# The opening of a hybrid RG-LRU / gMLP / ConvFFN layer: another order of loads, norms and first products

## The chip, the cores and the metric

One core of one Trainium2 chip runs the whole layer as one program. The metric is the device time of that program in microseconds, the median of several runs. Engines: PE is the matrix engine (PEld are its weight loads), DVE the vector engine, ACT the scalar engine, POOL the general engine, SP the engine from whose queue most transfers are issued.

## The reference, cut to what matters

One layer over 512 latent tokens and 256 context tokens of width 1024, all in float32. Only its beginning is touched by the change:

```python
def _rmsnorm(x, g):
    y = xf * lax.rsqrt(jnp.mean(xf * xf, axis=-1, keepdims=True) + EPS)
    return (y * g.astype(jnp.float32)).astype(x.dtype)

def _modulate(x, g, shift, scale):
    return _rmsnorm(x, g) * (1.0 + scale) + shift

m_x = (jax.nn.silu(c) @ w_mod[l] + b_mod[l]).reshape(B, N_MOD, 1, D_MODEL)
m_c = (jax.nn.silu(c_ctx) @ w_mod[l] + b_mod[l]).reshape(N_MOD, D_MODEL)
hc = _modulate(ctx, g_norm1[l], m_c[0], m_c[1])
pc = hc @ w_in[l][:, :W_R]                 # context: the 1280 recurrent columns only
hx = _modulate(x, g_norm1[l], m_x[:, 0], m_x[:, 1])
px = hx @ w_in[l]                          # latent: all 6912 columns
...                                        # convolution, gates, scans, gMLP, merge, FFN
```

So before the first product of the layer there have to be: the two vectors `c` and `c_ctx` put through silu and the first two blocks of `w_mod` (shift and scale), and the root mean square of each token. The latent scans start from the final context states, which is why the context products are wanted early too.

## The kernel before, in words

Tokens lie along the free axis and channels along the partitions, in 8 blocks (k = 0 to 7) of 128 channels: `xc[:, k, :]` holds 256 context tokens and then 512 latent tokens. Every large product is made in three passes: each float32 operand is split into a rounded high part and a rest (`wh`, `wl` for weights, `hxh`, `hxl` for the latent, `hch`, `hcl` for the context), and PE adds wh·xh, wh·xl and wl·xh in one PSUM bank. ACT casts the high part of a weight tile (line 93), DVE (POOL for some later tiles) subtracts to get the rest (line 95).

The order of instructions on each engine is made by a planner when the program is built: it takes what is ready by its own cost estimates, the earliest in program order first. `after(a, b)` adds an edge that only fixes the order of two instructions on one engine; it is no semaphore. A transfer waits in the queue of the engine that issues it; lines behind it on that queue wait too.

The opening, lines 214 to 348, goes as follows.

- Transfers from SP: the two condition rows (line 218), 1 MB of `w_mod` for block 0, the latent in eight pieces of 256 KB (line 228), the small parameters, `w_mod` for block 1, the first weight tile of two blocks, `w_mod` for block 2, the context, another weight tile, `w_mod` for block 3. POOL issues 512 KB of `c` spread over the partitions (`cbx`, line 352), which in the trace is its first transfer.
- `mod_cols(k)` (lines 257 to 273): 16 float32 matmuls of 128 columns on a quarter of the array's columns each give shift and scale of channel block k; ACT copies them out (line 268), one small matmul turns them (line 269), two DVE instructions add the bias and multiply by the norm's weight (lines 271 and 273). A float32 matmul stands in the trace as two instructions, so the 16 are 32.
- `norm_of` (lines 279 to 294): ACT squares each block, DVE adds the eight squares up (line 285), PE sums over the partitions with one matmul per 128 tokens against a column of ones (line 289), ACT takes the root, DVE the reciprocal, PE spreads the row over the partitions (line 203), ACT copies it to `rb` (line 294). First the latent, then the context.
- `mod_h(k, n)` (lines 325 to 330): DVE multiplies a block by scale and `rb`, ACT adds the shift and rounds to the high part, DVE makes the rest.
- The loop of lines 338 to 348: for each k, `mod_cols` and `mod_h` of block k + 2 (`LEAD = 2`) are issued ahead of the products of block k; the products are 18 passes of 512 latent columns into six banks (two `rx`, two `rg`, two `gr`) and 6 passes of 256 context columns into a shared bank (`rxc`).

Behind the loop the heads of the recurrent branch follow (`rx_head`, `gates_head`), whose first products are those of line 139. Weight tiles of 2 x 1024 columns go through two raw buffers and three pairs of split buffers for the whole kernel.

Of the kernel before, what the change touches and what calls it, by code (L numbers as in the profile page):

```python
# [10 lines left out]
F32 = mybir.dt.float32  # L11
F32R = mybir.dt.float32r
# [25 lines left out]
LEAD = 2  # L38
# [14 lines left out]
class Weights:  # L53
# [3 lines left out]
    def __init__(self, tc, raw, hl, ahead):  # L57
        self.tc, nc = tc, tc.nc
        self.nc, self.raw, self.hl, self.ahead = nc, raw, hl, ahead
        self.boost = 0  # L60
        self.units = []
        self.blocks = []
        self.loaded = 0
        self.split = 0
        self.taken = 0
        self.tiles = {}

# [8 lines left out]
    def load(self, u):  # L76
        while self.loaded <= u:
            src, n = self.units[self.loaded]
            t = self.raw.tile([P, 2 * BLK], F32, tag="raw", name=f"raw{self.loaded}")
            self.nc.sync.dma_start(t[:, :n], src)  # L80
            self.tiles[self.loaded] = t
            self.loaded += 1
        return self.tiles[u]

    def prepare(self, upto):
        nc = self.nc
        while self.split <= min(upto, len(self.blocks) - 1):
            u, at, n, on_pool, extra = self.blocks[self.split]
            r = self.load(u)[:, at : at + n]
            hl = self.extra if extra else self.hl  # L90
            h = hl.tile([P, BLK], F32R, tag="wh", name=f"wh{self.split}")
            l = hl.tile([P, BLK], F32R, tag="wl", name=f"wl{self.split}")
            nc.scalar.copy(h[:, :n], r)  # L93
# [14 lines left out]
def hybrid_block(ctx: ExitStack, tc: tile.TileContext, a: dict, out: bass.AP):  # L108
# [35 lines left out]
    for i in range(4):  # L144
        W.add(a["w_first"][i], [(4 + NFIRST) * P] * 2)
# [47 lines left out]

    def rstd_of(p, ss, tag, n=1, bias=None):
        r = p.tile([P, n], F32, tag=f"{tag}r", name=f"{tag}r", bufs=2)
        nc.scalar.activation(r, ss, AF.Sqrt, scale=1.0 / D, bias=eps if bias is None else bias)
        nc.vector.reciprocal(r, r)
        return r
# [14 lines left out]

    rx_ps, rg_ps = {}, {}

    with pool("pro", side="right") as pro:
        crow = pro.tile([2 * KD, P], F32, name="crow")
        nc.sync.dma_start(crow, a["c_row"])
        wms = {}

        def load_mod(k):
            wms[k] = pro.tile([P, 2, KD, P], F32, tag="wm", name=f"wm{k}", bufs=4)
            nc.sync.dma_start(wms[k].rearrange("p s k c -> p (s k c)"), a["w_mod01"][k])

        load_mod(0)
        xc = pro.tile([P, KD, TT], F32, name="xc")
        for k in range(KD):
            nc.sync.dma_start(xc[:, k, TC:], a["xc"][k])
        nc.sync.dma_start(sm, a["smalls"])
        load_mod(1)  # L230
        W.load(0)
        load_mod(2)
        nc.sync.dma_start(xc[:, :, :TC], a["ctx"].rearrange("p (k t) -> p k t", k=KD))
        W.load(1)
        load_mod(3)
# [6 lines left out]
        nc.gpsimd.memset(c32, 0.0)  # L242
        psc = mm_tile("psc")
        nc.tensor.transpose(psc[:, : 2 * KD], sig, ident[: 2 * KD, : 2 * KD])
        nc.vector.tensor_copy(c32[:, :, 0:2], psc[:, : 2 * KD].rearrange("p (n k) -> p k n", n=2))
        nc.vector.tensor_copy(sc, psc[:, :KD])
# [6 lines left out]
        nc.vector.tensor_copy(bm1[:, :, 0], col("bmod", 0, KD))  # L253
        nc.vector.tensor_scalar(bm1[:, :, 1], col("bmod", KD, KD), 1.0, None, op0=ALU.add)
        mss = {}

        def mod_cols(k):


            pm = aux_tile(f"pm{k}", 1)  # L260
            for kk in range(KD // 2):
                for s in range(2):
                    for h in range(2):
                        at = 64 * s + 32 * h
                        nc.tensor.matmul(pm[at : at + 32, :P], c32[:, 4 * h + kk, :], wms[k][:, s, 4 * h + kk, :],
                                         start=kk == 0, stop=kk == KD // 2 - 1, tile_position=(0, at))
# [3 lines left out]
            ms = mss[k] = pro.tile([P, 2, 2], F32, tag="ms", name=f"ms{k}", bufs=4)  # L270
# [5 lines left out]
        sqs = pro.tile([P, TT], F32, name="sqs")  # L276
        rb = pro.tile([P, TT], F32, name="rb")

        def norm_of(lo, hi):
            sq = lambda k: pro.tile([P, T], F32, tag="sq", name=f"sq{lo}{k}", bufs=4)[:, : hi - lo]  # L280
            nc.scalar.activation(sqs[:, lo:hi], xc[:, 0, lo:hi], AF.Square)
            for k in range(1, KD):
                q = sq(k)
                nc.scalar.activation(q, xc[:, k, lo:hi], AF.Square)
                nc.vector.tensor_tensor(sqs[:, lo:hi], sqs[:, lo:hi], q, op=ALU.add)
            n = (hi - lo) // P
            pss = aux_tile(f"pss{lo}", 0)
            for t in range(n):
                nc.tensor.matmul(pss[:, t : t + 1], sqs[:, lo + t * P : lo + (t + 1) * P], ones[:, 0:1],
                                 start=True, stop=True)  # L290
            r = rstd_of(pro, pss[:, :n], f"n1{lo}", n)
            prb = aux_tile(f"rb{lo}", 0)[:, : hi - lo]
            spread_rows(prb, r, n)
            return nc.scalar.copy(rb[:, lo:hi], prb)

        mod_cols(0)
        norm_of(TC, TT)
        mod_cols(1)
        normed = norm_of(0, TC)


        rxc = aux_tile("rxc", 0)
        gr_ps = {j: mm_tile(f"gr{j}") for j in range(NFIRST)}
        for j in range(2):
            rx_ps[j] = (mm_tile(f"rx{j}"), rxc[:, j * TC : (j + 1) * TC])
            rg_ps[j] = mm_tile(f"rg{j}")

        def products(k, wh, wl):
            xs = ((hxh[:, k, :], hxl[:, k, :]), (hch[:, k, :], hcl[:, k, :]))
            outs = [(rx_ps[j][0], j, *xs[0]) for j in range(2)] + [(rg_ps[j], 2 + j, *xs[0]) for j in range(2)]  # L310
            outs += [(gr_ps[j], 4 + j, *xs[0]) for j in range(NFIRST)] + [(rx_ps[j][1], j, *xs[1]) for j in range(2)]
            c0 = 4 + NFIRST
            for i, (o, j, xh, xl) in enumerate(outs):
                c = slice(j * P, (j + 1) * P)
                for n, (w, x) in enumerate(((wh, xh), (wh, xl), (wl, xh))):
                    first, last = k == 0 and n == 0, k == KD - 1 and n == 2
                    mm = nc.tensor.matmul(o, w[:, c], x, start=first and i != c0 + 1, stop=last and i != c0)
                    if (first or last) and i >= c0:
                        if i > c0:
                            after(mm, shared)  # L320
                        shared = mm

        PARTS = ((TC, TT, hxh, hxl), (0, TC, hch, hcl))

        def mod_h(k, n):
            lo, hi, dh, dl = PARTS[n]
            x, sh = xc[:, k, lo:hi], mss[k][:, n, 0:1]
            nc.vector.scalar_tensor_tensor(x, x, mss[k][:, n, 1:2], rb[:, lo:hi], op0=ALU.mult, op1=ALU.mult)
            nc.scalar.activation(dh[:, k, :], x, AF.Identity, bias=sh)
            nc.vector.scalar_tensor_tensor(dl[:, k, :], x, sh, dh[:, k, :].bitcast(F32), op0=ALU.add, op1=ALU.subtract)  # L330
# [3 lines left out]
        mod_h(0, 1)  # L334
        W.prepare(1)
        mod_h(1, 0)
        mod_h(1, 1)
        for k in range(KD):
            if k + 4 < KD:
                load_mod(k + 4)  # L340
            if k in (0, 2):
                W.load(k // 2 + 2)
            blk = W.take(ahead=1)
            if k + LEAD < KD:
                mod_cols(k + LEAD)
                mod_h(k + LEAD, 0)
                mod_h(k + LEAD, 1)
            products(k, *blk)

    W.boost = 1000  # L350

    nc.gpsimd.dma_start(cbx, a["c_b"])
# [20 lines left out]
    with pool("lamp") as lp:  # L373
# [4 lines left out]
        nc.vector.scalar_tensor_tensor(z, lam, -1.0, lam, op0=ALU.mult, op1=ALU.max)  # L378
# [270 lines left out]
    for k in range(KD):  # L649
        nc.gpsimd.dma_start(x1c[:, k, :], a["xc"][k])  # L650
# [207 lines left out]
def _layout(v):  # L858
# [7 lines left out]
    o["xc"] = f(np.asarray(v["x"][0]).T.reshape(KD, P, T))  # L866
# [66 lines left out]
```

## Time and profile before

| | us |
|---|---|
| median of 3 runs | 991.13 (991.07 to 996.96) |
| the profiled execution: its time | 989.86 |
| the profiled execution: its span | 988.1 |
| PE busy in the span | 951.6 (96%) |
| DVE busy | 665.2 (67%) |
| ACT busy | 478.0 (48%) |
| first product (line 317) starts | 24.68 |
| first product of the heads (line 139) starts | 75.51 |

"Busy" of PE counts every matmul until its modelled end, so that a busy PE can still be one that waits a little between passes. The span is what lies between the first and the last instruction; 1.8 us of the profiled time lie around it. A row of a timeline has start, duration, engine, line, what is written from what, the count of instructions merged, and in brackets the idle time of the engine before them with what ended it.

### The profile page before, as it was taken

The numbers are of one execution on the slowest core, as the hardware profiler recorded it, in microseconds if no ns is written. First come the engines' busy times: TensorE is split into PE (matmuls) and PEld (weight loads), VectorE is DVE, ScalarE is ACT, GpSimd is POOL, SyncE is SP. The second block draws the span as 40 slices with busy tenths as digits, with TensorE's granted clock in tenths as the row PEclk, the third lists the DMA queues.
The fourth block names the chain that finished last, engine by engine and source line by source line (L and its number), as shares of the span: only waits on it lengthen the run. The fifth ranks groups of instructions, "written<-read, shape, count | busy, mean of one in ns | idle before, by whom it ended". The sixth has DMA issues, their size and how long they took to land.

```text
span 988.1 us, 11916 instructions
## 1 busy us (share of the span) xinstructions
PE 951.6 (96%) x4787; PEld 789.4 (80%) x4787; DVE 665.2 (67%) x867; ACT 478.0 (48%) x661; POOL 95.0 (10%) x92
## 2 busy tenths in 40 slices
PE   3999999999999999999999998999999999999997
PEld 2788888888888788788888798888778888887686
DVE  3768496968574976586634456798886447888764
ACT  4546979786989552234222343443333213333333
POOL 0000000000000011100001031222220002222020
PEclk9999999999999999999999999999999999999999
DMA  9532212132222276734524331222213332221232
GB/s 355 223 134 86 78 51 86 43 107 86 86 86 86 86 257 233 257 148 175 198 97 170 111 125 43 86 86 86 85 43 108 105 128 86 85 86 64 84 109 86
DMA packets 23511, 116.85 MB, mean 118 GB/s; under 512 B 2576, under 2 KB 3744, under 8 KB 14368
## 3 DMA queue, kind: packets, MB, share of 16 engines
q1 hardware_dynamic: 17488, 94.59, 26.9%
q0 software_dynamic: 5968, 21.50, 6.2%
q8 instruction: 37, 0.61, 0.2%
q14 instruction: 18, 0.15, 0.1%
HBM read 113.98 MB, written 2.10 MB: 117 GB/s over the span
## 4 chain that ended last, share of the span: by engine, by line
PE 65%; DVE 16%; ACT 8%; issue 6%; DMA 3%; POOL 1%; SPq 0%; ACTq 0%; DVEq 0%; POOLq 0%
DVE acc L797 8%; PE d L140 4%; PE d L141 4%; PE d L139 4%; PE up L139 4%; PE up L141 4%; PE up L140 4%; DVE wl L95 2%; DMA wmod<-in_w_mod 2%; ACT wh L93 2%; PE pg L139 2%; PE pg L140 2%; PE pg L141 2%; PE gg L141 1%; PE gg L140 1%
## 5 line engine op out<-in xcount | busy, mean ns | idle before, releaser
L93 ACT CAST wh<-raw 128x1024 fp32r<-128x1024 f32 (+1 forms) x156 | 161.3, 1038 | 231.6 <-PE d L141 44.6
L95 DVE TENSOR_TENSOR wl<-raw,wh 128x1024 fp32r<-128x1024 f32 (+1 forms) x132 | 159.4, 1210 | 119.9 <-ACT wh L93 119.3
L797 DVE SCALAR_TENSOR_TENSOR acc<-gpad,sm,acc 128x512 f32<-128x512 f32 x176 | 159.4, 916 | 19.1 <-ACT acc L794 15.0
L141 PE MATMUL up<-h2h,wl 128*128 128x512 f32 (+1 forms) x384 | 145.1, 378 | 6.8 <-POOL wl L95 6.8
L139 PE MATMUL up<-h2h,wh 128*128 128x512 f32 (+1 forms) x384 | 144.8, 377 | 1.4 <-ACT wh L93 1.4
L140 PE MATMUL up<-h2l,wh 128*128 128x512 f32 (+1 forms) x384 | 143.9, 375 | 0.0
L141 PEld LDWEIGHTS up<-h2h,wl 128*128 128x128 f32 x384 | 73.2, 191 | 23.3 <-POOL wl L95 8.8
L95 POOL TENSOR_TENSOR wl<-raw,wh 128x1024 fp32r<-128x1024 f32 x24 | 61.2, 2552 | 292.4 <-ACT wh L93 280.4
L139 PEld LDWEIGHTS up<-h2h,wh 128*128 128x128 f32 x384 | 73.1, 190 | 14.8 <-ACT wh L93 2.9
L140 PEld LDWEIGHTS up<-h2l,wh 128*128 128x128 f32 x384 | 73.3, 191 | 12.5
L800 ACT ACTIVATE acc<-acc 128x512 f32<-128x512 f32 x22 | 13.9, 632 | 134.5 <-DVE acc L797 134.5
L140 PE MATMUL d<-wl,fh 128*128 128x512 f32 (+1 forms) x186 | 72.0, 387 | 0.1
L141 PE MATMUL d<-wh,fl 128*128 128x512 f32 (+1 forms) x186 | 71.1, 382 | 0.0
L139 PE MATMUL d<-wh,fh 128*128 128x512 f32 (+1 forms) x186 | 71.0, 382 | 0.0
L558 DVE SCALAR_TENSOR_TENSOR wmod<-wmod,cbx 128x1024 f32<-128x1024 f32 x24 | 29.2, 1222 | 27.4 <-DMA wmod<-in_w_mod 27.3
L140 PEld LDWEIGHTS d<-wl,fh 128*128 128x128 f32 x186 | 34.9, 188 | 8.8 <-DVE wl L95 1.4
L139 PEld LDWEIGHTS d<-wh,fh 128*128 128x128 f32 x186 | 34.9, 188 | 7.9
L141 PEld LDWEIGHTS d<-wh,fl 128*128 128x128 f32 x186 | 35.0, 188 | 7.2
L555 POOL DMA_DIRECT2D wmod<-in_w_mod x32 | 16.9, 528 | 246.4 <-DVE yrl L538 128.8
L474 DVE TENSOR_TENSOR i<-i,xr 128x768 f32<-128x768 f32 x20 | 18.9, 954 | 19.7 <-ACT i L467 19.7
L140 PE MATMUL pr<-yrl,wh 128*128 128x512 f32 x80 | 31.7, 396 | 0.0
L141 PE MATMUL pr<-yrh,wl 128*128 128x512 f32 x80 | 31.7, 396 | 0.0
(316 smaller groups left out, 2162.1 us busy)
## 6 DMA issues: line engine op xcount, KB each, us to landing
raw<-in_w_up SPq DMA_DIRECT2D x22, 1024.0 KB, 4.7
wmod<-in_w_mod POOLq DMA_DIRECT2D x32, 512.0 KB, 4.1
raw<-in_w_down SPq DMA_DIRECT2D x22, 512.0 KB, 3.2
wm<-in_w_mod SPq DMA_DIRECT2D x8, 1024.0 KB, 8.8
raw<-in_w_lru SPq DMA_DIRECT2D x5, 1024.0 KB, 4.7
raw<-in_w_pr SPq DMA_DIRECT2D x5, 1024.0 KB, 6.4
raw<-in_w_rx SPq DMA_DIRECT2D x4, 1024.0 KB, 4.8
raw<-in_w_rg SPq DMA_DIRECT2D x4, 1024.0 KB, 4.7
```

The source lines that it names most:

```text
L93: nc.scalar.copy(h[:, :n], r)
L95: eng.tensor_tensor(l[:, :n], r, h[:, :n].bitcast(F32), op=ALU.subtract)
L139: nc.tensor.matmul(o, wh, xh, start=first, stop=False)
L140: nc.tensor.matmul(o, wh, xl, start=False, stop=False)
L141: nc.tensor.matmul(o, wl, xh, start=False, stop=last)
L474: nc.vector.tensor_tensor(i[u], i[u], xr[h][:, u % 2, :], op=ALU.mult)
L555: nc.gpsimd.dma_start(wm, a["w_mod25"][n - 2, k])
L558: nc.vector.scalar_tensor_tensor(wm, wm, 1.0, cbx, op0=ALU.mult, op1=ALU.mult, accum_out=m)
L797: nc.vector.scalar_tensor_tensor(acc, pad[:, dy : dy + ROWS, dx : dx + GRID_W], col("ffw", 9 * i + q), acc, op0=ALU.mult, op1=ALU.add)
L800: nc.scalar.activation(accf, accf, AF.Gelu_apprx_tanh)
```

## The change

- The latent is fetched first, right behind the condition rows, in four transfers of 512 KB; then `w_mod` for block 0, the small parameters, the first weight tile (now one block, not two), and so on. All transfers of the opening, `cbx` too, go from SP, chained in a fixed order.
- While the data are under way, PE runs 16 float32 matmuls of 128 columns that nobody reads (`WARM`); the transposition of the condition rows stands behind the first four.
- The squares of the latent are made by ACT (even k) and DVE (odd k); PE adds them over the blocks too, with four matmuls for each k into one PSUM tile, and runs three more unread matmuls (`FILL`) between two blocks. All of these are chained. The table for the square root is loaded behind the last of ACT's squares by an instruction of its own.
- `mod_cols(0)` is queued behind these sums; `mod_cols(k + 1)` and `mod_h` of the latent for k + 1 follow the first of the six outputs of block k (`LEAD` is in effect 1).
- The eight weight blocks of the opening get split buffers of their own (`whl1`), so that all are kept. The context is normalised and multiplied after the latent's loop; its first product is queued behind the latent's products of block 5 (`CTX_AT`).
- Casts of weights are queued on ACT behind the latest `hxh`.
- The later re-read of the latent for the residual takes four transfers in place of eight.

The diff, cut to its core:

```diff
-LEAD = 2
+LEAD = 1
+WARM = 16
+FILL = 3
+CTX_AT = 5
...
+    FW = (4 + NFIRST) * P
+    for k in range(2):
+        W.add(a["w_first"][0][:, k * FW : (k + 1) * FW], [FW], extra=True)
+    for i in range(1, 4):
+        W.add(a["w_first"][i], [FW] * 2, extra=True)
...
+    exp, W.extra = opened("whl1", bufs=KD, side="right")
...
+        W.queued(nc.sync.dma_start(crow, a["c_row"]))
+            wms[k] = pro.tile([P, 2, KD, P], F32, tag="wm", name=f"wm{k}", bufs=3)
+        for i in range(4):
+            W.queued(nc.sync.dma_start(xc[:, 2 * i : 2 * i + 2, TC:], a["xc"][i].rearrange("p (k t) -> p k t", k=2)))
         load_mod(0)
+        W.queued(nc.sync.dma_start(sm, a["smalls"]))
+        W.load(0)
         load_mod(1)
+        W.load(1)
         load_mod(2)
...
+        for n in range(WARM):
+            if n == WARM // 4:
+                ahead = after(nc.tensor.transpose(psc[:, : 2 * KD], sig, ident[: 2 * KD, : 2 * KD]), ahead)
+            mm = nc.tensor.matmul(warm[:, :P], ident, ones, start=True, stop=True)
+            ahead = after(mm, ahead) if ahead else mm
...
+        def norm_x():
+            pss = aux_tile("pss", 0)
+            mm = ahead
+            for k in range(KD):
+                q = pro.tile([P, T], F32, tag="sq", name=f"sq{k}", bufs=4)
+                x = xc[:, k, TC:]
+                if k % 2:
+                    sq = nc.vector.tensor_tensor(q, x, x, op=ALU.mult)
+                    if k == 1:
+                        after(sq, copied)
+                else:
+                    squared = nc.scalar.activation(q, x, AF.Square)
+                for t in range(T // P):
+                    mm = after(nc.tensor.matmul(pss[:, t : t + 1], q[:, t * P : (t + 1) * P], ones1,
+                                                start=k == 0 and t == 0, stop=k == KD - 1 and t == T // P - 1), mm)
+                for _ in range(FILL if k < KD - 1 else 0):
+                    mm = after(nc.tensor.matmul(warm[:, :P], ident, ones, start=True, stop=True), mm)
+            after(nc.scalar.activation(pro.tile([P, 1], F32, name="root"), ones1, AF.Sqrt), squared)
+            r = rstd_of(pro, pss[:, : T // P], "n1x", T // P)
+            prb = aux_tile("rbx", 0)
+            spread_rows(prb, r, T // P)
+            return nc.scalar.copy(rb[:, TC:], prb), mm
...
+        spread, summed = norm_x()
+        hxs = [spread]
+        W.behind = lambda cast: after(cast, hxs[-1])
...
+        mod_cols(0, summed)
...
+        W.prepare(0)
+        mod_h(0, 0)
+        for k in range(KD):
+            blks.append(W.take(ahead=1 if k < KD - 1 else 0))
+            if k == 0:
+                W.load(2)
+            elif k == 2:
+                W.load(3)
+                W.queued(nc.sync.dma_start(xc[:, :, :TC], a["ctx"].rearrange("p (k t) -> p k t", k=KD)))
+            elif k == 3:
+                W.load(4)
+                W.queued(nc.sync.dma_start(cbx, a["c_b"]))
+            if k + 3 < KD:
+                load_mod(k + 3)
+            mm = products(k, *blks[k], OUTS[:1])
+            if k + 1 < KD:
+                mod_cols(k + 1, mm)
+                mod_h(k + 1, 0)
+            last = products(k, *blks[k], OUTS[1:])
+            if k == CTX_AT:
+                gate = last
+        normed = norm_ctx(lambda ins, k: after(ins, hxs[CTX_AT + 1 + k // 4]))
+        rxc = aux_tile("rxc", 0)
+        COUTS = [(rxc[:, j * TC : (j + 1) * TC], j, 1) for j in range(2)]
+        for k in range(KD):
+            mod_h(k, 1)
+            products(k, *blks[k], COUTS)
+        after(starts["c"], gate)
...
-    nc.gpsimd.dma_start(cbx, a["c_b"])
...
-    for k in range(KD):
-        nc.gpsimd.dma_start(x1c[:, k, :], a["xc"][k])
+    for i in range(4):
+        nc.gpsimd.dma_start(x1c[:, 2 * i : 2 * i + 2, :].rearrange("p k t -> p (k t)"), a["xc"][i])
```

`norm_ctx` is the old `norm_of` for the context alone: squares on ACT, sums over the blocks on DVE, two matmuls, root, reciprocal, spreading, copy.

## Rows read from the trace of the kernel before

**Rows 1.** Windows: stretch, length, busy time and count per engine, clock, DMA share, GB/s.

```profile
0.00:24.68 24.68, 8.95 (x86) 7.32 (x86) 7.45 (x20) 10.37 (x18) 1.93 (x11) 1.00 0.94 355
24.68:75.51 50.83, 50.39 (x405) 39.70 (x405) 34.32 (x79) 27.09 (x50) 0.25 (x6) 1.00 0.47 180
```

**Rows 2.** The chain of work that ended last, to 26 us: start, length, what.

```profile
2.12 6.91 DMA xc<-in_xc
...
15.23 1.88 PE pss L289 x8
...
17.18 1.28 ACT L196
...
19.01 2.08 PE rb L203 x8
21.09 1.91 PE pm L265 x32
```

**Rows 3.** PE's timeline at the end of the first loop.

```profile
59.64 1.08 PE L265 MATMUL pm<-wm,c 128*32 128x128 f32 x32
...
65.87 0.40 PE L317 MATMUL rx<-hxh,wh 128*128 128x512 f32 x1
...
69.97 0.28 PE L317 MATMUL rxc<-hch,wh 128*128 128x256 f32 x1
...
70.69 0.40 PE L317 MATMUL rx<-hxh,wh 128*128 128x512 f32 x1
```

**Rows 4.** A window at the start, for the transfers (last column GB/s).

```profile
0.00:10.00 10.00, 0.25 (x1) 0.18 (x1) 0.57 (x2) 3.17 (x5) 1.93 (x11) 1.00 0.78 286
```

**Rows 5.** PE's timeline, float32 passes of 128 columns among others.

```profile
410.36 1.05 PE L612 MATMUL s<-wst,vg 128*128 128x128 f32 x8
411.17 0.47 PE L139 MATMUL u<-hxh,wh 128*128 128x512 f32 x1
```

**Rows 6.** PE's timeline, second half's norm: one-column sums behind idle time.

```profile
602.71 0.58 PE L685 MATMUL qss<-ones,sqs 128*128 128x1 f32 x4 [2.85 <-DVE sqs L679]
```

**Rows 7.** Windows around it (clock is the third figure from the end).

```profile
604.00:605.00 1.00, 1.00 (x7) 1.00 (x7) 0.00 (x0) 0.00 (x0) 0.58 (x1) 0.50 0.03 8
...
607.00:608.00 1.00, 1.00 (x11) 1.00 (x10) 1.00 (x3) 0.46 (x2) 0.00 (x0) 1.00 0.00 0
```

**Rows 8.** Timeline, the two passes of the small matmul in the opening, early and later.

```profile
12.92 0.50 PEld L269 LDWEIGHTS pm<-sel,mrow 128*128 128x128 f32 x2 [0.90 <-issue]
...
23.34 0.30 PEld L269 LDWEIGHTS pm<-sel,mrow 128*128 128x128 f32 x2 [0.84 <-ACT mrow L268]
```

**Rows 9.** Groups by line and shape, to 76 us: busy, mean ns, idle before.

```profile
L95 DVE TENSOR_TENSOR wl<-raw,wh 128x768 fp32r<-128x768 f32 x8 | 7.5, 953 | 0.4 <-ACT wh L93 0.4
...
L328 DVE SCALAR_TENSOR_TENSOR xc<-xc,ms,rb 128x512 f32<-128x512 f32 x8 | 6.0, 751 | 2.9 <-ACT rb L294 2.8
...
L329 ACT ACTIVATE hxh<-xc,ms 128x512 fp32r<-128x512 f32 x8 | 5.8, 723 | 5.5 <-DVE xc L328 5.5
...
L328 DVE SCALAR_TENSOR_TENSOR xc<-xc,ms,rb 128x256 f32<-128x256 f32 x8 | 3.7, 479 | 1.5 <-ACT rb L294 1.5
...
L268 ACT COPY mrow<-pm 128x128 f32<-128x128 f32 x8 | 2.1, 257 | 7.2 <-PE pm L265 7.2
L273 DVE TENSOR_SCALAR ms<-ms,sm 128x2 f32<-128x2 f32 x8 | 1.8, 219 | 0.1
```

**Rows 10.** PE's timeline, the context's norm inside the first loop.

```profile
36.48 0.60 PE L289 MATMUL pss<-ones,sqs 128*128 128x1 f32 x4
...
37.92 0.71 PE L203 MATMUL rb<-ident,n10r 128*128 128x128 f32 x4
```

**Rows 11.** Timeline of the opening, POOL's and ACT's part.

```profile
1.12 0.29 POOL masks.py:199 TENSOR_SCALAR_AFFINE_SELECT ident<-ident 128x128 f32<-128x128 f32 x1
...
9.05 3.23 ACT L284 ACTIVATE sq<-xc 128x512 f32<-128x512 f32 x5 [1.22 <-DMA xc<-in_xc]
...
21.12 0.58 ACT L294 COPY rb<-rb 128x512 f32<-128x512 f32 x1 [2.38 <-PE rb L203]
```

More of the change, by code (lines that the diff above doesn't have):

```diff
@@ L60, in __init__ @@
         self.boost = 0
+        self.behind = self.last = None
+        self.chain = None
         self.units = []
@@ L66, in __init__, with queued @@
         self.tiles = {}
+    def queued(self, dma):
+        if self.chain is not None:
+            if self.last is not None:
+                self.chain(dma, self.last)
+            self.last = dma
     def add(self, src, sizes, on_pool=False, extra=False):
@@ L90, in prepare @@
             hl = self.extra if extra else self.hl
-            h = hl.tile([P, BLK], F32R, tag="wh", name=f"wh{self.split}")
-            l = hl.tile([P, BLK], F32R, tag="wl", name=f"wl{self.split}")
-            nc.scalar.copy(h[:, :n], r)
+            h = hl.tile([P, n], F32R, tag="wh", name=f"wh{self.split}")
+            l = hl.tile([P, n], F32R, tag="wl", name=f"wl{self.split}")
+            cast = nc.scalar.copy(h[:, :n], r)
+            if self.behind is not None:
+                self.behind(cast)
             eng = nc.gpsimd if on_pool else nc.vector
@@ L192, in hybrid_block @@
     nc.gpsimd.memset(eps, EPS)
+    inverse = {}
     def rstd_of(p, ss, tag, n=1, bias=None):
@@ L252, in hybrid_block, with mod_cols @@
         bm1 = pro.tile([P, KD, 2], F32, name="bm1")
-        nc.vector.tensor_copy(bm1[:, :, 0], col("bmod", 0, KD))
-        nc.vector.tensor_scalar(bm1[:, :, 1], col("bmod", KD, KD), 1.0, None, op0=ALU.add)
         mss = {}
-        def mod_cols(k):
+        def mod_cols(k, behind):
             pm = aux_tile(f"pm{k}", 1)
@@ L288, in norm_of, with norm_ctx @@
+        def norm_ctx(late):
+            sqs = pro.tile([P, TC], F32, name="sqs")
+            late(nc.scalar.activation(sqs, xc[:, 0, :TC], AF.Square), 0)
+            for k in range(1, KD):
+                q = pro.tile([P, T], F32, tag="sq", name=f"csq{k}", bufs=4)[:, :TC]
+                late(nc.scalar.activation(q, xc[:, k, :TC], AF.Square), k)
+                nc.vector.tensor_tensor(sqs, sqs, q, op=ALU.add)
+            n = TC // P
+            pss = aux_tile("pssc", 0)
             for t in range(n):
-                nc.tensor.matmul(pss[:, t : t + 1], sqs[:, lo + t * P : lo + (t + 1) * P], ones[:, 0:1],
-                                 start=True, stop=True)
@@ L291, in norm_of @@
-            r = rstd_of(pro, pss[:, :n], f"n1{lo}", n)
-            prb = aux_tile(f"rb{lo}", 0)[:, : hi - lo]
+                nc.tensor.matmul(pss[:, t : t + 1], sqs[:, t * P : (t + 1) * P], ones1, start=True, stop=True)
+            r = rstd_of(pro, pss[:, :n], "n1c", n)
+            prb = aux_tile("rbc", 0)[:, :TC]
             spread_rows(prb, r, n)
[L294 to L299, printed above, removed]
@@ L314, in products @@
                 c = slice(j * P, (j + 1) * P)
[L315 to L319, printed above, removed]
+                for m, (w, x) in enumerate(((wh, xs[n][0]), (wh, xs[n][1]), (wl, xs[n][0]))):
+                    first, last = k == 0 and m == 0, k == KD - 1 and m == 2
+                    mm = nc.tensor.matmul(o, w[:, c], x, start=first and (n == 0 or j == 0), stop=last and (n == 0 or j == 1))
+                    if (first or last) and n:
+                        if j:
@@ L320, in products @@
                             after(mm, shared)
                         shared = mm
+                        if first and not j:
+                            starts["c"] = mm
+            return mm
+        OUTS = [(rx_ps[j], j, 0) for j in range(2)] + [(rg_ps[j], 2 + j, 0) for j in range(2)]
+        OUTS += [(gr_ps[j], 4 + j, 0) for j in range(NFIRST)]
         PARTS = ((TC, TT, hxh, hxl), (0, TC, hch, hcl))
@@ L333, in hybrid_block @@
         mod_h(0, 0)
[L334 to L337, printed above, removed]
+        blks = []
         for k in range(KD):
[L339 to L348, printed above, removed]
+            blks.append(W.take(ahead=1 if k < KD - 1 else 0))
[23 more added lines that the diff above has]
+        after(starts["c"], gate)
+        for j in range(2):
+            rx_ps[j] = (rx_ps[j], COUTS[j][0])
+        W.prepare(KD + 1)
+        W.chain = W.behind = None
+    exp.close()
     W.boost = 1000
-    nc.gpsimd.dma_start(cbx, a["c_b"])
     with pool("cb") as cp:
```

66 lines of the change are left out of this document (27 added, 39 removed).

## The prediction

> **What bounds the kernel now.** I read the windows of the whole span first: PE is busy 952 of 988 us, and from 24.68 us on it hardly pauses (50.39 busy of 50.83 us in the stretch of the first products [rows 1]). The change touches only what lies before 75.51 us, so its worth is the time by which the first product of the heads starts earlier or later; behind it PE carries the difference to the end. Ahead of 24.68 us PE is busy for only 8.95 us [rows 1]. There the chain of waits tells the story [rows 2]: the latent, behind 1 MB of `w_mod`, until 9.03 us; squares and their sum on DVE until 15.2; eight passes against the column of ones (1.88 us); a table load of 1.28 us on ACT; spreading (2.08 us); `mod_cols` (1.91 us); then scaling and rounding. The reader should see that PE's parts in it run at half rate: 32 passes of `mod_cols` take 1.91 us there and 1.08 us at 59.64 [rows 2, 3]. The clock's column reads 1.00 all the same in that stretch, so I go by durations.
>
> **PE's prices.** One step k of the first loop is 4.82 us of products (65.87 to 70.69), 4.10 of them latent; a step with `mod_cols` takes 6.23 (59.64 to 65.87), so `mod_cols` costs 1.41 [rows 3]. A float32 matmul of 128 columns (two passes) costs 0.20 us at the upper level: four in 0.81 us, from 410.36 to 411.17 [rows 5]. At the lower level it is 0.47 (1.88 / 4) for a one-column sum and 0.52 (2.08 / 4) for 128 columns [rows 2]. The change makes 16 unread matmuls, 32 sums and 21 fillers. For a matmul of the last two kinds I take 0.22, near the long row of rows 5; the far end is 0.30, from two sums in 0.60 us with their tail [rows 10].
>
> That low price rests on eight passes with eight different weights, 0.10 us each, so the loads are hidden [rows 5]. The Trainium skill (TensorE: Matmul & The Clock Gate, section "Part 3: Packing small matmuls — row/col tiling") says the contrary: a weight load overlaps a running matmul only where the two use different rows of the array. By that page's figures a pass would take about 0.16 us (an estimate), the 106 passes 17.0 us and the kernel 995; the trace disagrees.
>
> **The sum, step by step.**
>
> 1. *Latent first.* In the first 10 us the transfers ran at 286 GB/s [rows 4], 2.86 MB, all behind 2.1 us [rows 2], so 0.36 MB per us. The latent is 2.1 MB: landed at 2.1 + 5.8 = 7.9 us, or 9 if `w_mod` interleaves. A square on ACT is 0.65 us (3.23 / 5) [rows 11]; ACT and DVE share them, so the last is done by 9 to 10 us. What is displaced, `w_mod` 0 and the first weight tile, lands by 12 us, before its use. The queue of SP takes `cbx` too; its users come behind the context's norm.
> 2. *Unread matmuls.* They can start when `ident` is written, 1.41 us [rows 11]; say 1.5. The clock: PE worked from 19.01 on at half rate, and at 23.34 the same two loads that took 0.50 at 12.92 take 0.30 [rows 2, 8]; after the pause at 599.9 the work began at 602.71 and the clock read 1.00 again in the window from 607 [rows 6, 7]. Both times the upper level was back about 4 us after the work began, so I take it at 5.7 us. Until then 7.5 matmuls at 0.52 and the transposition are done, the other 8.5 take 1.9: end at 7.6 us.
> 3. *Sums and fillers.* 53 x 0.22 = 11.7 us, chained: end at 19.3 us (18.2 at 0.20, 23.5 at 0.30). The squares are ready long before, so PE is late here, not the transfers. Before, the sums ended at 17.1 [rows 2]: this step loses 2.2 us. DVE's seven additions go, and nobody on the path wins by it.
> 4. *From sums to first product.* Before: 24.68 - 17.1 = 7.6 us. The table load (1.28) moves ahead under the sums; spreading and `mod_cols(0)` run at the upper level, about 1.0 and 1.08 us on one engine in either order. Spreading last: root and reciprocal hide under `mod_cols`, rows spread at 2.1, `rb` copied (0.58 [rows 11]) at 2.7, scaling 0.75, rounding 0.72 [rows 9]: 4.2 us. Spreading first: `mod_cols` ends at 2.1, then copy 0.26, turning 0.35, two DVE steps 0.4, scaling and rounding 1.5, with hand-overs 5.0. Middle 4.6: first product at 23.9, a gain of 0.8 us. Casting the first weight tile (under 0.85 us) lies under the scaling.
> 5. *First stage.* Before 50.83 us [rows 1] = 8 x 4.82 + 6 x 1.41 + 3.8; of the 3.8 the context's norm is 1.3 [rows 10], the rest waits. After: 38.56 + 7 x 1.41 (one more `mod_cols` lies inside) + 1.3 + 0.5 = 50.2. The 0.5 is the start: DVE owes the low part of `hx` (0.75, as for the scaling) and of the weights (0.95) [rows 9], PE has six passes of 0.23 to bridge. Gain 0.6.
> 6. *Context last* costs nothing: it is eight scalings and eight rests of 0.48 [rows 9] on DVE, 7.7 us, behind `hxh` of block 6, with about 17 us of latent products and context products over them. Without that cover the wait would be up to 3 us. Eight kept weight tiles cost only memory; the pads of the first head wait for the context's first products, still 5 us before they are wanted.
> 7. *Residual in four transfers*: POOL's issue, hidden under PE, 0; if not, tenths.
>
> Sum: 0.8 + 0.6 = 1.4 us less, 988.5 of the profiled 989.86. The median of the runs shown lies 1.27 above that execution, so **989.7**.
>
> **Rivals.**
>
> - *The clock falls in the pause.* Between spreading and first product PE has only the small turning matmul for some 2 us. After 2.85 us of idling the clock read 0.50 [rows 6, 7] until about 607: some 3.2 us at half rate, 1.6 us lost; against it, the pause is shorter here. 991.3. The Trainium skill (the same page, section "Why this matters for your kernels") warns of such gaps between bursts; rows 7 shows it, no row shows it for so short a pause at the upper level.
> - *Steps come late.* With a lead of 1, `hxh` of the next block needs 0.7 (first output) + 1.08 + 0.26 + 0.35 + 0.4 + 0.75 + 0.72, with hand-overs 4.7 us, of a step of 5.5. If a weight rest of 0.95 and the other half of a scaling stand ahead on DVE, the step is late by 0 to 0.95; at 0.6, seven times: 993.9 (996.4 at most). For it: DVE is busy 34 of 51 us in this stage [rows 1]. Against: casts are queued right behind `hxh`, in the slack.
> - *Dear passes.* The sums' loads do not hide, 0.30 per matmul [rows 10]: 4.2 us more, 993.9. The skill's page on loads, cited above, would lead this way.
> - *The order is not what the text says.* The edges fix little; the planner mixes the context in or delays a cast, and the old waits of 2 us come back: 991.7.
> - *Slower: the clock never rises under the sums.* One-column matmuls and their loads may not lift it. Warm-up to 10.1, 53 x 0.47 = 24.9: sums end at 35.0, 15.7 us later, 1005.4. It is slower by over 1% once 45 of the 53 run at the low level. For it: the sums at 15.23 and 19.01 ran low. Against: rows 8.
> - *Faster: sums keep pace with the landing.* They end at 10 instead of 19.3: 980.4. It would need 0.05 us per matmul, below any row.
>
> **Numbers.** About 1% (9.9 us) is what a measurement of this kernel tells from no change. Forecast 0.40, clock falls in the pause 0.20, late steps 0.14, dear passes 0.08, other order 0.08, clock low 0.06, pace with the landing 0.04. The forecast's own ends: 1.1 less at 0.20 per matmul, 0.4 less for the order, 0.5 less waiting, and 2 either way for a new plan behind the opening: 985.7. The upper end is that of late steps, 996.4. Range 985.5 to 996.5, which leaves out the last two rivals and some tail. Faster 0.05, within 1% 0.88, slower 0.07.
>
> **What would show it.** Sums' last matmul at 19.3 us and squares done before 10 (step 3); no table load between sums and root; first product at 23.9; first product of the heads at 74.1 instead of 75.51; sums of four in 0.9 us. Sums of four in 1.9 us, a first product after 26, or waits of PE at each `hxh` would make the prediction wrong.

## The result and the profile after

The changed kernel takes **1000.66 us** (median; 995.94 to 1006.55), the kernel before in the same comparison 991.03: ratio 1.0093, interval 1.0072 to 1.0114. 989.7 was forecast, 996.5 was the top of the range. The profiled execution took 1005.51 us, one of the longer ones; a second profile, taken later, 1001.38.

From the profile's page of the changed kernel (span 1003.7 us): the engines' busy time, and the clock in 40 slices of 25.1 us:

```profile
PE 971.8 (97%) x4917; PEld 807.7 (80%) x4917; DVE 662.3 (66%) x864; ACT 476.7 (47%) x658; POOL 93.0 (9%) x87
...
PEclk9998999999999999999999998999999999999999
```

PE is 20 us busier (971.8 for 951.6). Part of that is unread matmuls, and part is work at a lower clock: the fourth slice's digit is an 8. Where this lies is seen best in windows cut at the marks of the opening (columns as in rows 1):

```profile
0.00:25.31 25.31, 20.64 (x181) 19.65 (x181) 5.62 (x15) 8.11 (x14) 1.29 (x10) 1.00 0.68 254
25.31:33.00 7.69, 7.69 (x54) 5.62 (x55) 3.48 (x6) 2.37 (x4) 0.00 (x0) 0.78 0.82 314
33.00:70.34 37.34, 37.34 (x329) 28.34 (x328) 23.28 (x41) 14.92 (x29) 0.32 (x6) 1.00 0.64 238
70.34:73.62 3.28, 1.21 (x9) 0.93 (x7) 1.24 (x4) 1.19 (x4) 0.00 (x0) 1.00 0.67 275
73.62:81.30 7.68, 7.43 (x48) 7.18 (x48) 5.70 (x16) 5.50 (x10) 0.00 (x0) 0.78 0.01 2
81.30:83.42 2.12, 0.17 (x2) 0.00 (x0) 1.71 (x5) 2.11 (x5) 0.00 (x0) 1.00 0.00 0
83.42:91.00 7.58, 7.58 (x28) 6.16 (x29) 7.53 (x19) 6.33 (x10) 0.00 (x0) 0.77 0.00 0
```

The first product comes at 25.31 us (24.68 before), the first product of the heads at 83.42 (75.51 before [rows 1]). The reader should see a pattern of three: a stretch in which PE stands (2.25 us before 25.31, most of 70.34 to 73.62, 81.30 to 83.42), and behind each one a window of about 7.6 us whose granted clock is 0.77 or 0.78 on the mean: some 3.4 us at 0.50 (1.2 GHz), the rest at 1.00. Before, none of this stage's windows is under 1.00. PE's timeline gives the three pauses and their releasers:

```profile
25.31 0.73 PE L370 MATMUL rx<-hxh,wh 128*128 128x512 f32 x2 [2.25 <-ACT hxh L388]
...
26.57 0.63 PE L370 MATMUL rx<-hxl,wh 128*128 128x512 f32 x1
...
70.11 0.39 PE L370 MATMUL gr<-hxh,wl 128*128 128x512 f32 x1
70.34 0.50 PE L342 MATMUL pssc<-ones,sqs 128*128 128x1 f32 x4
71.39 0.71 PE L224 MATMUL rbc<-ident,n1cr 128*128 128x128 f32 x4 [0.55 <-DVE n1cr L218]
73.62 0.40 PE L370 MATMUL rxc<-hch,wh 128*128 128x256 f32 x1 [1.52 <-ACT hch L388]
...
77.00 0.41 PE L370 MATMUL rxc<-hcl,wh 128*128 128x256 f32 x1
...
77.84 0.28 PE L370 MATMUL rxc<-hcl,wh 128*128 128x256 f32 x1
...
83.42 0.50 PE L155 MATMUL rx<-hxh,wh 128*128 128x512 f32 x1 [1.95 <-ACT pad L500]
```

The second pause is the context's norm: its sums start at 70.34, right behind the last latent product at 70.11. DVE had added up the squares by 63.4 us, so what held the sums was their place in PE's order (the first experiment tests it). From 73.62 on the context products follow each other at 0.21 us, from 77.5 on at 0.12. The third is the first head waiting for room in PSUM, until ACT has copied `rxc` and `rx` out to the pads (PE's releaser is `pad`). ACT's timeline says what it did instead:

```profile
77.81 0.91 ACT L388 ACTIVATE hch<-xc,ms 128x256 fp32r<-128x256 f32 x2 [1.07 <-DVE xc L387]
78.74 1.28 ACT L432 ACT_TABLE_LOAD   x1
80.03 1.06 ACT L432 ACTIVATE cs<-cbx 128x1024 f32<-128x1024 f32 x1
81.11 1.28 ACT L456 ACT_TABLE_LOAD   x1
82.40 0.22 ACT L456 ACTIVATE z<-z 128x20 f32<-128x20 f32 x1
82.53 0.35 ACT L499 COPY pad<-rxc 128x256 f32<-128x256 f32 x1
82.78 0.59 ACT L500 COPY pad<-rx 128x512 f32<-128x512 f32 x1
```

Two table loads, the sigmoid of `c` over 1024 columns and a small exponential stand ahead of the copies, 3.84 us, all behind the context's last `hch`. In the kernel before the same sigmoid runs inside the loop:

```profile
40.35 1.06 ACT L355 ACTIVATE cs<-cbx 128x1024 f32<-128x1024 f32 x1
```

**The account**, from the forecast's own marks. Head product 83.42 against a forecast of 74.1: 1.4 for the first product (25.31 for 23.9); 7.69 x 0.22 = 1.7 for the clock behind it; 0.55 + 1.52 + 0.24 = 2.3 for the context's norm (the last of these stands before the second context product); 7.68 x 0.22 = 1.7 for the clock behind that; 1.95 for the pads; 0.3 left over. Another 7.58 x 0.23 = 1.7 lies behind the head product. Together 11.1; 989.7 + 11.1 = 1000.8, the median is 1000.66. That it comes so near is in part luck, since the pieces are those of one execution. In the second profile the first product comes at 26.40, the clock reads 0.50 from about 25 us, already within the pause, until beyond 31, about twice as long as above, and the head product comes at 85.39:

```profile
25.00:26.00 1.00, 0.00 (x0) 0.00 (x0) 0.59 (x1) 0.38 (x1) 0.00 (x0) 0.50 0.72 117
26.40:31.40 5.00, 5.00 (x39) 3.49 (x40) 1.66 (x2) 0.81 (x2) 0.00 (x0) 0.50 0.80 327
```

Against the kernel before, the first profile is 7.9 us later at the head product and 9.6 at the first `v` product (313.1 for 303.5), the second 9.9 and 11.6 (315.1). In the first, the longer execution, 4.5 more come between `v` and `gg`:

```profile
418.31 1.23 DVE L635 SCALAR_TENSOR_TENSOR wmod<-wmod,cbx 128x1024 f32<-128x1024 f32 x1 [3.94 <-DMA wmod<-in_w_mod]
```

DVE stands at a transfer twice (4.02 us at 441.18), and the rests of weights queued behind it are late for PE (waits of 1.20 and 2.44 us at the `u` products; the kernel before has one of 1.1 there). The second profile of the same kernel has no such wait there.

### The profile page after: what moved, and what is told of

It is laid out like the page before. It is cut to its first block, busy times and chain, and to the rows that moved or that the text cites. A ratio compares the mean times of both kernels' runs of the same rounds, so it can differ in the third digit from the quotient of the medians.

```text
span 1003.7 us, 12148 instructions
## 1 busy us (share of the span) xinstructions
PE 971.8 (97%) x4917; PEld 807.7 (80%) x4917; DVE 662.3 (66%) x864; ACT 476.7 (47%) x658; POOL 93.0 (9%) x87
## 4 chain that ended last, share of the span: by engine, by line
PE 61%; DVE 18%; issue 9%; ACT 8%; DMA 2%; POOL 2%; ACTq 0%; POOLq 0%; DVEq 0%
DVE acc L874 9%; PE d L156 4%; PE d L155 4%; PE d L157 4%; PE up L157 3%; PE up L155 2%; PE up L156 2%; DVE wl L111 2%; DMA wmod<-in_w_mod 2%; ACT wh L107 2%; PE pg L156 1%; PE pg L155 1%; PE pg L157 1%; PE gg L157 1%; PE gg L156 1%
```

## The experiments

Three theories. **P**: the two pauses made by the context's place, with the slow stretch behind each, are the loss. **S**: it is the sums and fillers ahead of the first product. **D**: it is later, where transfers collide in the `u` stage. Comparisons were made on several chips, so ratios to the kernel before are compared; 0.001 is 1 us.

**Context's norm earlier.** Only the call moves, into the loop.

```diff
         for k in range(KD):
             ...
+            if k == 6:
+                normed = norm_ctx(...)
             last = products(k, *blks[k], OUTS[1:])
-        normed = norm_ctx(...)
```

> Theories: P = the loss lies in two pauses of PE made by the context standing last (its norm at 70.3 us, and the eviction of the first products at 81.3 us behind ACT's silu of c), each with a stretch at the lower clock behind it. S = the loss comes from the unread matmuls, sums and fillers ahead of the first product. D = the loss comes later, where the new plan lets transfers collide in the u stage. Here the context's norm is put in program order before the rest of the latent's products of block 6; nothing else. P: the pause from 70.3 to 73.6 and the half-rate stretch behind it go, 3 + 1.7 us, so 995 to 997 instead of 1000.7, the wait for the eviction at 81 stays. S and D: no change, 1000 or more.

995.88 us, ratio 1.0055 (1.0034 to 1.0077): 3.8 us less than the changed kernel's 1.0093. The second pause and its slow stretch are gone (70 to 75 at 1.00), the third stays (2.31 us), with 0.66 behind it:

```profile
70.00:75.00 5.00, 5.00 (x40) 4.80 (x39) 5.00 (x11) 3.08 (x5) 0.00 (x0) 1.00 0.02 3
...
80.00:85.00 5.00, 5.00 (x16) 3.92 (x16) 4.95 (x13) 4.96 (x7) 0.00 (x0) 0.66 0.00 0
```

By the account this pause is worth 2.3 + 1.7 = 4.0.

**Silu of `c` and softplus later.** The block of ACT's work ahead of the pads is moved behind the first gates.

```diff
-    with pool("cb") as cp:   # sigmoid of cbx, product; softplus of lam behind it
-        ...
+    rg_head(0) ...           # first gate's sigmoids
+    after(nc.scalar.activation(cs, cbx, AF.Sigmoid), normed)
+    nc.vector.tensor_tensor(cbx, cbx, cs, op=ALU.mult)
+    ...                      # softplus of lam
```

> ACT's silu of c and the softplus of the decays (two table loads, 3.9 us on ACT) are moved in program order behind the evictions of the first head; the context's norm stays last. P: the 1.95 us wait before the first product of the heads and the half-rate stretch behind it go, 2 + 1.7 us: 996 to 998. S and D: no change.

996.59 us, ratio 1.0069 (1.0049 to 1.0089), 2.4 us less, where the account has 1.95 + 1.7. About 1 us comes back further on: PE's waits for ACT at the gates' products `gc` are 1.8 us here and 0.8 in the changed kernel. The head product comes at 80.85 without a wait, at full rate; the second pause stands:

```profile
71.09 0.71 PE L224 MATMUL rbc<-ident,n1cr 128*128 128x128 f32 x4 [0.55 <-DVE n1cr L218]
73.32 0.58 PE L370 MATMUL rxc<-hch,wh 128*128 128x256 f32 x1 [1.52 <-ACT hch L388]
...
80.85 0.40 PE L155 MATMUL rx<-hxh,wh 128*128 128x512 f32 x1
```

**Both.**

> The context's norm early and the silu late, both at once; the context's products stay last. P: both pauses and the half-rate stretches behind them go: 995.9 and 996.6 against 1000.7 make 4.8 and 4.1, together 8.9, so 991 to 993; what is left above the kernel before is the half-rate stretch behind the pause ahead of the first product. S: no better than either edit alone, 995 or more.

992.60 us, ratio 1.0022 (1.0014 to 1.0031): the two edits together save 7.1 us of the 9.3, as P says. One slow stretch is left, at the start:

```profile
25.00:30.00 5.00, 4.38 (x39) 3.01 (x40) 1.69 (x2) 1.56 (x3) 0.00 (x0) 0.67 0.86 352
```

**No fillers** (`FILL = 0`), for S.

> No fillers between the blocks of the sums (FILL = 0), all else as changed. The 21 fillers took 0.25 us each by the changed kernel's trace, so the sums should end at about 14 us instead of 19.1, and the first product come at 20 to 21 instead of 25.3. S: the time falls by 4 to 5 us or more, to 991 to 996, and that is the greater part of the loss. P: it falls by at most 4 to 5 us and the two pauses at 70 and 81 us stay, still slower than the kernel before. If the clock falls without the fillers, the sums take 0.47 each and nothing is gained.

999.03 us, ratio 1.0099 (1.0076 to 1.0121): nothing is won. Without the 42 passes the 64 of the sums take 0.17 us each on the mean (0.10 with them), and they end at 19.4, where they ended before: the clock reads 1.00 until 11 us and 0.50 from 12 us on:

```profile
8.42 11.09 PE L321 MATMUL pss<-ones,sq 128*128 128x1 f32 x64
19.44 1.93 PE L291 MATMUL pm<-wm,c 128*32 128x128 f32 x32
...
26.54 1.22 PE L370 MATMUL rx<-hxh,wh 128*128 128x512 f32 x2 [2.22 <-ACT hxh L388]
```

```profile
8.42:11.00 2.58, 2.58 (x26) 2.58 (x25) 0.69 (x1) 0.63 (x1) 0.00 (x0) 1.00 1.04 429
12.00:19.40 7.40, 7.40 (x36) 7.40 (x35) 0.69 (x1) 1.38 (x2) 0.00 (x0) 0.50 0.92 375
```

PE was busy all the while: one-column sums alone did not keep the upper level, 128-column fillers between them did. So the fillers cost nothing that these runs show, and S, as "take them out", falls.

**Context in the loop as before** (its load moved ahead, its norm at k = 2, its products with each k).

> Undoes 'context last' alone: the context is loaded behind w_mod of block 2, normalised in the loop at k = 2, and its products follow the latent's of each block, as in the kernel before; latent first, sums on PE, fillers and kept tiles stay. P: both pauses go, first product of the heads at about 76 us, total 990 to 993, no different from the kernel before. S: nothing changes, 1000. D: the later stall in the u stage stays or goes by chance, 990 to 996.

993.34 us, ratio 1.0043 (1.0024 to 1.0061), a little over what was expected, as is the head product (79.23 for about 76). The pause at 70 is gone. But although the context's norm is done by 49 us here, silu of `c` still runs at 75.84, and of the wait for the pads 1.33 us are left (no slow stretch follows it); the slow stretch at 25 to 30 us stands (0.66). So the late norm alone is not what holds silu back.

**Room for the silu**, on top of the context in the loop. A new theory, R: the sigmoid's buffer has no place but where the opening's pool lay.

```diff
-                q = pro.tile([P, T], F32, tag="sq", name=f"sq{k}", bufs=4)
+                q = pro.tile([P, T], F32, tag="sq", name=f"sq{k}", bufs=2)
 ...                                 # the same for csq; softplus block ahead of the silu, its pool kept open
```

> The kernel with the context in the loop (993.34 us; head product at 79.23 behind a wait of 1.33 us for the pads, silu of c at 75.84 on ACT), with two buffers for the squares in place of four, which frees 4 KB per partition beside the opening's pool, and with the softplus block ahead of the silu. Theory R (room): the sigmoid's buffer of 4 KB had to lie where the opening's pool lay, because the eight kept weight tiles left no other place, so silu of c could not run before the last hcl, however early the context's norm. With room it runs near 50 us inside the loop, as it did at 40.3 in the kernel before; the wait for the pads goes and the head product comes at 77.5 to 78.2: 991.3 to 992.5 us, ratio to the kernel before 1.002 to 1.003. Rival: silu is late because of its place behind the loop in program order; it stays at 75 us and the wait at 1.3, 993 to 994.

993.29 us, ratio 1.0031 (1.0017 to 1.0044): by its median no gain, by the ratio 1.2 us, with intervals that overlap. The trace decides: both pieces run inside the loop, and the head product comes at 77.70 without a wait, where R put it. The three edits were not run one by one. The addresses that the tiles get when the programs are built agree with R: the sigmoid's buffer lies at bytes 97248 to 101344 of a partition in the kernel before, the changed one and the one with the context in the loop. The opening's pool begins at 137856 in the first and, with 49152 bytes of kept weight tiles beside it, at 98784 in the other two; with two square buffers it begins at 102880, behind the sigmoid's buffer.

```profile
51.03 0.22 ACT L439 ACTIVATE z<-z 128x20 f32<-128x20 f32 x1
...
54.66 1.06 ACT L454 ACTIVATE cs<-cbx 128x1024 f32<-128x1024 f32 x1
```

With eight unread matmuls in the pause before the first product as well (as below):

> The same with eight unread matmuls behind the first turning matmul, so that the clock holds through the pause before the first product. With R the head product comes at 75.7 to 76.3, no stretch under 1.00 up to 90 us, 989.5 to 991, ratio 1.000 to 1.001, no better than the kernel before. Rival, gain given back later: 991 to 992.

991.96 us, ratio 1.0022 (1.0006 to 1.0039), which is where the rival put it. No window up to 90 us is under 1.00, but the head product comes at 77.04, later than expected, behind that of the kernel before (the first product comes at 26.42 in this profile): with the context in the loop and 21 fillers and 32 sums ahead, the opening is not shorter.

**Fillers in the pause before the first product**, on top of both edits: eight unread matmuls behind the small turning matmul of `mod_cols(0)`.

```diff
-        mod_cols(0, summed)
+        mm = mod_cols(0, summed)      # returns the turning matmul
+        for _ in range(8):
+            mm = after(nc.tensor.matmul(warm[:, :P], ident, ones, start=True, stop=True), mm)
```

> As the kernel with both edits, and eight unread matmuls more in the pause of 2.25 us between the last matmul of mod_cols(0) and the first product. The first product should stay at 25.3 us; if the fall of the clock behind that pause (25.9 to 29.4 us at half rate) comes from PE's idling, it goes, and the kernel gains 1.5 to 2 us against the kernel with both edits. If the clock falls all the same, or the eight delay the first product, nothing is gained.

992.25 us, ratio 1.0012 (1.0003 to 1.0021). The slow stretch is gone, with the pause cut to 0.36 us:

```profile
22.71 2.03 PE L358 MATMUL warm<-ones,ident 128*128 128x128 f32 x16
25.11 0.73 PE L373 MATMUL rx<-hxh,wh 128*128 128x512 f32 x2 [0.36 <-ACT hxh L391]
```

```profile
25.00:30.00 5.00, 4.89 (x49) 3.76 (x50) 2.83 (x5) 1.20 (x4) 0.00 (x0) 1.00 0.98 369
```

The head product comes at 76.44 instead of 78.48, but only 1.0 us by the ratios, 0.35 by the medians, arrives at the end, less than the 1.5 to 2 expected. In this profile a wait of 1.3 us in the `u` stage came back, which the kernel with both edits has not; one profile of each does not show that it is the rule.

**`mod_cols(0)` between the last sums**, in place of the fillers behind blocks 5 and 6, and `mod_cols(1)` behind the spreading, on top of both edits.

> As the kernel with both edits; besides mod_cols(0) runs between the sums of blocks 6 and 7, in place of the fillers behind blocks 5 and 6, and mod_cols(1) in the pause behind the spreading, with a lead of 2 from there on. First product at 23 to 23.5 instead of 25.3, one mod_cols (1.4 us) less in the first stage, no long pause: 3.5 to 5 us less than with both edits, 986 to 989, faster than the kernel before by 1 to 4 us.

989.45 us (985.81 to 997.46), ratio 1.0000 (0.9979 to 1.0021), no better than the kernel before, though the first product comes at 24.61 and the head product at 74.37. The last 24 passes of the sums, without fillers but with the 32 of `mod_cols(0)` between them, and waits of PE at 19 us were followed by half rate from 20 us on (0.50 in the windows from 20 to 23), here in the spreading, which takes 2.08 instead of 1.16 us:

```profile
18.22 1.05 PE L327 MATMUL pss<-ones,sq 128*128 128x1 f32 x8
...
19.90 2.08 PE L224 MATMUL rbx<-ident,n1xr 128*128 128x128 f32 x8 [0.40 <-DVE n1xr L218]
```

**The changed kernel again**, for D.

> The changed kernel once more, for a second trace. If the 3.6 us of waiting in the u stage and the half-rate stretch behind it (4.5 us in the first trace) are part of its plan, they are here again; if they come by chance of the transfers, this run may be without them and is then nearer to 996 than to 1005.

999.91 us, ratio 1.0090 (1.0072 to 1.0108); its profile took 1001.38. It has both pauses of the context and no wait in the `u` stage, and is 11.5 us longer than the profile of before all the same, a lead that the kernel before has at the first `v` product already (11.6). So D accounts for the difference between the two profiles, and not for the loss. That an execution without the wait would be nearer to 996 than to 1005 did not come true for this one.

**Half the sums**, for the part of S that is left: DVE adds the squares of two blocks, PE sums four pairs with 16 matmuls and nine fillers.

```diff
                 else:
                     squared = nc.scalar.activation(q, x, AF.Square)
+                    even = q
+                    continue
+                nc.vector.tensor_tensor(q, q, even, op=ALU.add)
                 for t in range(T // P):
```

> The changed kernel with one edit: DVE adds the square of each even block to that of the next odd block, so TensorE sums four pairs with 16 one-column matmuls instead of 32, with three fillers between the pairs (9 instead of 21). Theory N: the sums on TensorE are what holds the first product back, and the rest of the opening follows them unchanged. Four times 0.95 and three times 0.75 us behind the unread matmuls' end at 7.2 put the sums' end at 13 instead of 19.2, the first product at 19 to 20 instead of 25.3: 994 to 997 us against 1000.7. Rival: the weights and w_mod set the pace once the products start earlier (the transfers run at over 400 GB/s until 15 us): waits of PE appear inside the first loop, and the time stays at 998 to 1001. Both pauses made by the context's place stay in either case.

995.37 us, ratio 1.0057 (1.0036 to 1.0079): 3.6 us less. The sums end at 14.5 us (13 was expected) and the first product comes 4.6 us earlier, behind a pause of the same length; no wait for weights appears in the loop. Both pauses of the context stay; the pads' grows to 2.95 us. Part of the gain may be chance: in this profile no slow stretch follows the context's norm, though its waits (0.55, 1.52 and 0.26 us) are those of the changed kernel:

```profile
13.65 0.95 PE L324 MATMUL pss<-ones,sq 128*128 128x1 f32 x8
...
20.67 1.22 PE L373 MATMUL rx<-hxh,wh 128*128 128x512 f32 x2 [2.26 <-ACT hxh L391]
```

```profile
69.39:77.07 7.68, 6.21 (x47) 5.80 (x47) 5.70 (x14) 5.50 (x9) 0.00 (x0) 1.00 0.00 0
```

**Half the sums on top of both edits and the fillers in the pause.**

> The same edit on top of three others: context normed within the loop ahead of block 6's later products, silu of c and softplus moved behind the first gate, eight unread matmuls in the pause before the first product (that kernel without the pairs took 992.25, its first product of the heads came at 76.4). Theory N: the first product and the first product of the heads come 5 to 6 us earlier, 70 to 71.5; 986 to 988.5 us, faster than the kernel before (991.1). Rival, transfers set the pace: first product early, but waits for w_mod or weights inside the loop, first product of the heads at 75 to 76, 990.5 to 992.5.

988.72 us (984.45 to 992.35), ratio 0.9988 (0.9968 to 1.0008). The head product comes at 71.62, 3.9 us before that of the kernel before, at full clock:

```profile
71.62 0.50 PE L155 MATMUL rx<-hxh,wh 128*128 128x512 f32 x1 [0.91 <-ACT am L562]
```

The end of the program shows only 1.2 us of it, within what can be told from none. Runs of this kernel lie 8 us apart, those of the kernel before in the same comparison 7 (985.89 to 992.87). The profiles show one thing in which executions differ. In all 14, PE waits 2.75 to 2.91 us for the second half's norm ([rows 6] has that of the kernel before). Behind it no slow stretch comes in three, one of some 3.4 us in seven, the kernel before among them, and one of some 6.8 us in four: this kernel, the one with room and fillers in the pause, and both profiles of the changed kernel. The first 7 us behind the wait, in the kernel with the context's norm earlier, the kernel before and this one (the clock is the third figure from the end):

```profile
606.80:613.80 7.00, 6.96 (x57) 6.87 (x58) 4.78 (x13) 3.25 (x8) 1.23 (x2) 1.00 0.00 0
602.71:609.71 7.00, 7.00 (x46) 7.00 (x47) 4.25 (x12) 3.13 (x8) 1.23 (x2) 0.76 0.00 1
598.66:605.66 7.00, 7.00 (x33) 7.00 (x34) 3.62 (x10) 2.50 (x7) 1.23 (x2) 0.51 0.00 0
```

From the first `up` product, 9 us ahead of the end of this wait, to the end of the program the three kinds take 392, 394 and 395.6 us. So this kernel is 4.1 us ahead of the kernel before at that product (589.9 for 594.0) and 2.4 at the end of its profile. What decides between the three kinds no run shows, nor which of them the runs without a profile had; so it stays open whether this version beats the kernel before.

## Why the prediction was wrong

**The step that failed is step 6**, "Context last costs nothing". Its cover was counted right (17 us of products) and its dependences were not followed to PE. The scalings and rests that it spoke of wait for `rb`, and `rb` comes from two matmuls and a spreading on PE; the planner takes what is ready in program order, `norm_ctx` is called behind the loop, so these stood behind all latent products, and no latent product was left to lie over the chain root, reciprocal, spreading, copy, scaling, rounding. "Without that cover the wait would be up to 3 us" was the right size (2.3 us) for the case that came. The second claim of that step, "Eight kept weight tiles cost only memory", failed too: memory was the price. They took the room in which silu of `c` had run beside the opening, so it waited for the opening's last `hcl` and then stood, with the softplus, ahead of ACT's copies to the pads, "still 5 us before they are wanted". Giving back 4 KB moved it from 75.84 to 54.66 us. The two pauses with the slow stretches behind them are 2.3 + 1.7 + 1.95 + 1.7 = 7.7 us by the account; the two edits that take them away save 7.1. This is the greater part of the miss of 11.

**Steps 1 to 3 hold.** Unread matmuls ended at 7.4 (forecast 7.6), the sums at 19.2 (19.3), four of them 0.95 us long; in the second profile both ends are 1.1 us later. Four sums and three fillers take 1.57 us (7.36 to 8.93), 0.22 each as taken, with a weight load for every pass; no dear passes came. The squares were done at 13.7, not by 10, since four buffers let them run only as far ahead as PE; that costs nothing, as PE has no wait there. The loss of 2.2 us that the forecast saw is there, and it need not be: with half the sums the first product comes 4.6 us earlier.

**Step 4 was mis-sized**: 6.1 us (19.2 to 25.31) for 4.6. "Casting the first weight tile (under 0.85 us) lies under the scaling" is wrong; on both engines the work on this tile stands ahead:

```profile
21.56 0.83 ACT L107 CAST wh<-raw 128x768 fp32r<-128x768 f32 x1
22.29 0.27 ACT L296 COPY mrow<-pm 128x128 f32<-128x128 f32 x1
```

```profile
22.43 0.96 DVE L111 TENSOR_TENSOR wl<-raw,wh 128x768 fp32r<-128x768 f32 x1 [2.47 <-ACT wh L107]
23.30 0.15 DVE L299 TENSOR_TENSOR ms<-pm,bm 128x4 f32<-128x4 f32 x1
```

PE's part of `mod_cols` is over at 21.8, and its copy waits for the cast until 22.29; the small step on DVE waits for the rest of the weights until 23.30. The planner put the spreading between two parts of `mod_cols`, so that PE is done with both 2.5 us behind the sums: of the forecast's two orders it is the dearer one, of 5.0 us, and the casts come on top.

**Step 5** held within the loop (33 to 70.34: no wait of PE, clock 1.00), so the rival of late steps did not come. Its start did not hold: **the rival of the falling clock came true**, near its forecast price (1.6; 1.7 in the first profile, about twice that in the second), and twice more at pauses that the forecast had not seen. The price is not a fixed one: the pause of 2.85 us from which the forecast took it is followed by no slow stretch in three of the 14 profiles. The Trainium skill (TensorE: Matmul & The Clock Gate, section "Why this matters for your kernels") warns of gaps between bursts of matmuls, but of longer ones; here the clock fell behind waits of 2.25 and 1.95 us too.

**Step 7** could not be seen: no wait of PE at the residual's transfers in either profile. The chances put 0.20 on the falling clock and 0.08 on an order that the text does not say; both came at once, and their sum lay outside a range whose rivals had been priced one at a time.

## What to carry to other kernels

Work moved to the end of a loop is hidden only if its first step on the busy engine is queued ahead of the loop's last work: follow each chain to that engine, and price it twice, once as a wait and once as half rate behind it, which came behind most of these pauses and not behind all. Buffers that are newly kept take room from whatever ran beside them: ask what now has to wait for a pool to close, and whether it then stands ahead of the copies that free PSUM. Where a pause can't be avoided, unread matmuls can be put into it: in the three kernels here that have them, no slow stretch followed.

## What the runs showed of the hardware

- In the first 90 us of the changed kernel and its variants, pauses of PE of 1.81 to 2.95 us, and of 0.55 and 1.52 us close together, were followed by work at 0.50 (1.2 GHz), with one exception: in the kernel with half the sums, 0.55, 1.52 and 0.26 us were followed by 1.00. Single waits of 0.91 to 1.33 us at the head product were not followed by a fall.
- The length of a pause alone does not say what follows. Behind 2.25 us the clock was low for some 3.4 us in one profile of the changed kernel and for about twice as long in the other; behind 2.75 to 2.91 us not at all, for some 3.4 or for some 6.8 us. The `up` products wait four times for 1.28 to 1.71 us in each of the 14 profiles, and behind one of the four, not the same in all, the clock fell. In the kernel before, behind two waits of 1.70 us:

```profile
711.29:714.29 3.00, 3.00 (x13) 2.50 (x14) 2.86 (x5) 0.00 (x0) 0.00 (x0) 1.00 0.70 208
736.25:739.25 3.00, 3.00 (x8) 2.38 (x9) 2.86 (x5) 0.00 (x0) 0.00 (x0) 0.55 0.54 175
```

- One-column float32 matmuls, back to back on a busy PE from 8.42 us on, ran at 1.00 until 11 us and at 0.50 from 12 us; with three 128-column matmuls behind each four of them the same sums ran at 1.00.
- A fall of the clock need not show within the pause: in the window of 70.34 to 73.62 the column reads 1.00 with PE mostly idle, and the price stands in the window behind it. In the second profile of the changed kernel it reads 0.50 from 25 to 26 us, with PE idle.
